# Program order on all engines through the chunked scan of a decoder layer: later tanh, exponentials in four parts, recurrence between the conv taps, sample-state product on GpSimd

## The chip, the cores and the metric

One NeuronCore of one Trainium2 chip runs the whole layer as one program. The metric is the device time in microseconds (us). The kernel before was run three times: 1119.72, 1119.86 and 1118.34 us, median 1119.72. Engines are called as in the profile: PE is TensorE, DVE is VectorE, ACT is ScalarE, POOL is GpSimd, SP is SyncE, whose queue issues nearly all DMAs.

## What is computed

One layer of a hybrid decoder for 512 prompt tokens and 8 single-token samples (520 columns in all), `D_MODEL` 1024. The part that matters is the input projection and the SSD branch:

```python
proj = h @ w_in                              # u | z | xBC | dt | gates
xbc  = silu(conv_b + sum_k full[:, k:k+L] * conv_w[k])     # 4 taps, causal
dt   = softplus(dt_raw + dt_bias);  dA = dt * A            # 32 heads
# chunks of 128 tokens, 8 groups of 4 heads, state 128, head width 64
Acs  = cumsum(dA);  decay = exp(tril(Acs[l] - Acs[s]))
y_diag = (C B^T * decay) @ (x * dt)
state  = B^T @ (exp(Acs[-1] - Acs) * x * dt);  h[c+1] = h[c] * exp(Acs[-1]) + state
y = y_diag + (C * exp(Acs)) @ h + D * x      # then gated by silu(z)
# samples: y_s = C . (ssm state) + ..., one step each
```

After it come the gates, the projection, the output projection and a SwiGLU FFN.

## The kernel before

Weights and activations are split into a high and a low part (`hi`, `lo`), and each product is three matmuls: hi*hi, hi*lo, lo*hi. A *column* is one 128-wide column of outputs: 8 row tiles x 3 products x 2 halves of 260 tokens = 48 matmuls into a two-bank PSUM tile `m` (`main()`, two buffers). For each column a weight tile of 128x1024 is loaded (`raw`, three buffers, SP queue), cast on ACT (`whi`, L116) and its remainder taken on DVE (`wlo`, L117). `plan` is a list of functions with their weights; `perform()` calls them in turn, having made the weights of two columns ahead (`LOOK`). PE's instructions stand in program order (`manual_schedule`). So do those of ACT, DVE and POOL, but only in `start()`, up to about 55 us of the span; behind it a scheduler orders ACT, DVE, POOL and SP by its own priorities, with `urgent()` as a boost.

The scan runs over 8 groups `g`. A group has four conv columns, `x0`, `x1` (the two x tiles, conv columns 2g and 2g+1), `bb` (B, 16+g) and `cc` (C, 24+g), and two gate columns `zz` of the group before (2g-2, 2g-1). Group 0's x0, x1 and the dt column are computed in `start()`. After a conv column `conv()` does this: ACT copies the PSUM tile to `xb` (L614) and writes `v` = last tap + bias (L615), which together free the PSUM tile; POOL clears three columns of `xb` (L610), keeps conv state (L616, L617) and adds the samples' part (L618); DVE adds three taps (L620); ACT takes tanh (L621); DVE writes the result `dst` (L622); POOL keeps its sample columns (L623). `v` and `t` have two buffers, `xb` three.

`ssd_open()` runs `dt_parts()` (softplus as a polynomial, 16 small DVE operations up to the cumulative sum `acs`, L543 to L556), stores `acs` to DRAM, and prepares `cpre` for the samples on POOL (L588, L590: five operations on 128x256, after the load of `cvs`). `dec_load(g)` loads `acs` broadcast to 128 partitions (`dec`, 1 MB). `scan(g)` is a generator whose parts are put between the columns of the next group: the exponentials (`cd`, `ce`, 16 Relu of 128x128, one Exp of 128x2048; L649 to L656) and C*exp (L658); transposes of x and B with `xdt`, `xde`, `bm` (L671 to L683); C B^T with mask and decay (L688 to L694); the chunk states and their recurrence on POOL and DVE (L702 to L715); the two y products (L727, L729); last the samples: a transpose of the sample B and C rows `bc_s` (L737), their store to `dbc`, loads of the state `h0` and of `cc`, and 16 fused multiply-and-sum operations `jk` on DVE (L749).

The PSUM buffers that set the order are these two pools; `main()` takes an `m` tile, `bank()` a `b` tile:

```python
    pm = ctx.enter_context(tc.tile_pool(name="pm", bufs=2, space=bass.MemoryType.PSUM))
    pb = ctx.enter_context(tc.tile_pool(name="pb", bufs=4, space=bass.MemoryType.PSUM))
```

## Time and profile before

| | |
|---|---|
| times of three runs | 1118.34, 1119.72, 1119.86 us |
| the profiled execution's own time | 1117.87 us |
| its span in the trace | 1116.1 us |
| PE, DVE, ACT, POOL busy | 1077.5, 699.5, 452.6, 318.2 us |
| DMA | 165.36 MB, mean 148 GB/s |
| stages on PE | start to 55.7 us; rest of the prologue and group 0 of the scan to 106.5; z columns of group 1 on to 383; pooling columns to 460; gates, projection, output to 740; FFN to 1116 |

The prediction reads four views. The page gives each engine's busy time. The *windows* view gives it for stretches of the span, with the clock that PE was granted. The *chain* is the work that ended last, followed back in time. The *timeline* and *lines* views give single instructions or groups: start, duration, engine, line, output<-inputs, shapes, and in brackets the idle time ahead of it and what ended that. Busy matmuls overlap their successor, so lost PE time is best read from start to start.

### The profile page before, as it was taken

To read this page: it belongs to the slowest core of one execution; us is meant where nothing else is said; L and a number is where in the kernel's file an instruction comes from. 1 tells how busy PE (TensorE), PEld (TensorE's weight loads), DVE (VectorE), ACT (ScalarE), POOL (GpSimd) and SP (SyncE) were. 2 spreads that over 40 slices of the span, in tenths; PEclk is the share of its full clock that TensorE was granted. 3 is DMA by queue.
4 is the path that set the end of the run, shared out by engine and by line. 5 is a ranking of instruction groups with operands and counts; after the bars stand their busy time and mean duration, and the time that the engine had idled before them with its cause. 6 is when DMAs were issued, how large, how long until landed. Compare 5 with 4: busy or idle time off the path is not lost.

```text
span 1116.1 us, 22431 instructions
## 1 busy us (share of the span) xinstructions
PE 1077.5 (97%) x9345; PEld 1047.7 (94%) x9345; DVE 699.5 (63%) x1203; ACT 452.6 (41%) x734; POOL 318.2 (29%) x482
## 2 busy tenths in 40 slices
PE   8999999999999899999999999999999999999995
PEld 6898989999999899999999999899999999999995
DVE  5687787687787887889677745657554553323332
ACT  3266554645545534665433323532222222222220
POOL 1154223122221222000000000399999950000001
PEclk8999999999999999999999999999999999999998
DMA  9535543444445332554335446267666652223212
GB/s 363 199 101 157 152 116 118 136 142 134 144 128 150 122 123 83 199 157 168 132 136 177 142 144 217 95 207 221 203 209 208 194 176 85 86 90 97 85 53 77
DMA packets 58470, 165.36 MB, mean 148 GB/s; under 512 B 10881, under 2 KB 16513, under 8 KB 57601
## 3 DMA queue, kind: packets, MB, share of 16 engines
q1 hardware_dynamic: 51712, 142.96, 39.4%
q0 software_dynamic: 6656, 20.98, 6.1%
q8 instruction: 73, 1.20, 0.4%
q14 instruction: 29, 0.23, 0.1%
HBM read 151.05 MB, written 12.86 MB: 147 GB/s over the span
## 4 chain that ended last, share of the span: by engine, by line
PE 70%; DMA 10%; DVE 8%; ACT 4%; issue 3%; POOL 3%; SPq 0%; DVEq 0%; ACTq 0%; POOLq 0%
PE m L129 62%; DMA dbc<-bcs 5%; DMA cc<-dbc 4%; PE b L129 4%; DVE v L620 3%; DVE jk L749 2%; ACT whi L116 1%; PE b L287 1%; PE b L193 1%; PE b L727 1%; DMA dec<-dacs 1%; DVE wlo L117 1%; ACT xb L614 1%; PE b L729 1%; POOL hst L714 0%
## 5 line engine op out<-in xcount | busy, mean ns | idle before, releaser
L129 PE MATMUL m<-hh,whi 128*128 128x260 f32 (+1 forms) x1840 | 381.1, 287 | 15.0 <-ACT v L615 12.9
L129 PE MATMUL m<-hl,whi 128*128 128x260 f32 (+1 forms) x1840 | 374.2, 283 | 3.3 <-DVE hl L467 3.1
L129 PE MATMUL m<-hh,wlo 128*128 128x260 f32 (+1 forms) x1840 | 373.8, 283 | 0.0
L117 DVE TENSOR_TENSOR wlo<-raw,whi 128x1024 fp32r<-128x1024 f32 (+2 forms) x169 | 229.7, 1361 | 152.5 <-ACT whi L116 148.8
L116 ACT CAST whi<-raw 128x1024 fp32r<-128x1024 f32 (+2 forms) x169 | 173.3, 1028 | 368.1 <-PE m L129 248.2
L129 PEld LDWEIGHTS m<-hh,whi 128*128 128x128 f32 x1840 | 285.4, 189 | 23.6 <-ACT v L615 15.8
L129 PEld LDWEIGHTS m<-hl,whi 128*128 128x128 f32 x1840 | 285.1, 189 | 4.4 <-DVE hl L467 4.0
L129 PEld LDWEIGHTS m<-hh,wlo 128*128 128x128 f32 x1840 | 285.5, 189 | 0.0
L327 POOL TENSOR_TENSOR r<-me,mhalf 128x5 f32<-128x5 f32 (+2 forms) x6 | 6.4, 1066 | 436.6 <-DVE me L326 436.6
L620 DVE SCALAR_TENSOR_TENSOR v<-xb,cwh,v 128x512 f32<-128x512 f32 x96 | 80.9, 843 | 24.7 <-ACT v L615 24.0
L621 ACT ACTIVATE t<-v 128x520 f32<-128x520 f32 x32 | 20.4, 639 | 112.9 <-DVE v L620 100.4
L129 PE MATMUL m<-ah,whi 128*128 128x260 f32 x264 | 53.2, 283 | 0.0
L129 PE MATMUL m<-ah,wlo 128*128 128x260 f32 x264 | 53.1, 282 | 0.0
L129 PE MATMUL m<-al,whi 128*128 128x260 f32 x264 | 53.0, 282 | 0.0
L129 PE MATMUL m<-gh,whi 128*128 128x260 f32 x256 | 52.8, 288 | 0.0
L129 PE MATMUL m<-gl,whi 128*128 128x260 f32 x256 | 51.3, 282 | 0.0
L129 PE MATMUL m<-gh,wlo 128*128 128x260 f32 x256 | 51.3, 282 | 0.0
L1180 DVE TENSOR_TENSOR fs<-m,fs 128x520 f32<-128x520 f32 (+2 forms) x23 | 15.5, 676 | 56.6 <-PE m L129 55.8
L1167 POOL TENSOR_TENSOR ht<-bb,xds 128x512 f32<-128x512 f32 x32 | 46.2, 1443 | 2.5 <-DMA bb<-dbc 2.0
L749 DVE SCALAR_TENSOR_TENSOR jk<-h,cc 128x128 f32<-128x128 f32 x128 | 37.5, 293 | 12.8 <-DMA cc<-dbc 11.5
L1169 POOL TENSOR_TENSOR hs<-hs,ht 128x512 f32<-128x512 f32 x32 | 44.5, 1389 | 0.8
L129 PEld LDWEIGHTS m<-gh,whi 128*128 128x128 f32 x256 | 39.2, 188 | 2.6 <-PE b L287 1.3
(297 smaller groups left out, 1721.1 us busy)
## 6 DMA issues: line engine op xcount, KB each, us to landing
raw<-in_win SPq DMA_DIRECT2D x73, 512.0 KB, 3.6
raw<-in_wfi SPq DMA_DIRECT2D x44, 512.0 KB, 4.4
araw<-in_wada SPq DMA_DIRECT2D x24, 512.0 KB, 4.1
h<-in_sssm SPq DMA_DIRECT2D x16, 512.0 KB, 4.1
raw<-in_wssd SPq DMA_DIRECT2D x16, 512.0 KB, 3.4
hs<-in_sssm POOLq DMA_DIRECT2D x32, 256.0 KB, 4.2
out_ssms<-hs POOLq DMA_DIRECT2D x32, 256.0 KB, 3.8
raw<-in_wfo SPq DMA_DIRECT2D x16, 512.0 KB, 3.5
```

What stands on the lines that cost most here:

```text
L116: nc.scalar.copy(hi, raw)
L117: nc.vector.tensor_tensor(lo, raw, hi.bitcast(F32), ALU.subtract)
L129: nc.tensor.matmul(o, a[:, k, c0 : c0 + P], b[:, t0:t1], start=f, stop=e)
L193: nc.tensor.matmul(ps[32 * i : 32 * i + 32, 0:n], sc[:, k], raw[:, n * i : n * i + n], start=first, stop=last)
L287: nc.tensor.matmul(ps[32 * i : 32 * i + 32, 0:256], scr[:, k], w[:, 256 * i : 256 * i + 256], start=k == 0 and j == 0, stop=k == KD - 1 an ...
L614: nc.scalar.copy(shape(xb[:, 3 + t0 : 3 + t1]), o)
L620: nc.vector.scalar_tensor_tensor(v[:, 0:TP], xb[:, k : k + TP], w(k), v[:, 0:TP], ALU.mult, ALU.add)
L621: nc.scalar.activation(t, v, AF.Tanh, bias=0.0, scale=1.0)
L749: nc.vector.scalar_tensor_tensor(jk, h0[:, i, j], 1.0, cc[:, i], ALU.mult, ALU.mult, accum_out=y_s[:, 2 * g + j, b + i : b + i + 1],)
L1167: nc.gpsimd.tensor_tensor(t, bb.unsqueeze(2).broadcast_to([P, 2, 2, P]), at(xds), ALU.mult)
L1169: nc.gpsimd.tensor_tensor(h, h, t, ALU.add)
L1180: nc.vector.tensor_tensor(view(s[:, t0:t1]), u, view(s[:, t0:t1]), ALU.mult)
```

## The change

Line numbers in the diff's own text are those of the two files; the changed file's lines are some 10 to 140 higher. It does seven things.

1. `manual_schedule` for PE, ACT, DVE and POOL holds from `start()` to the end of the scan's loop, and for SP from group 0's `cc` on. Everything there stands in the order of the calls.
2. `conv()` no longer ends its own column: tanh, `dst` and the sample copy go into `late`, and the next column's `conv()` or `gate()` runs them after its own PSUM reads and taps (`flush`).
3. The exponentials of a group are four pieces (`decays`), called from the `bb` column on; the even groups' `ce` lies in `aa`.
4. The chunk states follow the `bb` column, their POOL and DVE steps between its three taps (`mix`); the decay products (`scores`) are split in two.
5. The samples have a generator `sample(g)` of their own: the transpose of `bc_s` first, then per four samples a load, one 128x1024 product on POOL and one DVE reduction instead of eight `jk`.
6. `dt_parts` becomes a generator in three pieces, called in `ssd_open`, after x1 and after bb of group 0.
7. `ahead` loads the raw weights of two more columns, and `start()` casts the first two weights itself.

The core of the diff:

```diff
+    def ahead(n, m=0):
+        queue, made, raws = W["queue"], W["made"], W["raws"]
+        for i in range(len(made), min(n, len(queue))):
+            ...
+                raw = raws.pop(i) if i in raws else load(src)
+                made.append(parts(raw, pool))
+        for i in range(len(made), min(n + m, len(queue))):
+            ...
+                raws[i] = load(u[0] if isinstance(u, tuple) else u)
...
-            while len(made) < min(at + len(us) + (LOOK if at else 0), len(queue)):
-                u = queue[len(made)]
-                made.append(unit(*u) if isinstance(u, tuple) else unit(u))
+            ahead(at + len(us) + (LOOK if at else 0), W.get("loads", 0))
...
-        with urgent():
-            dt_parts(sp)
+        S["dt"] = dt_parts(sp)
+        next(S["dt"])
...
+        if mix:
+            next(mix)
         for k in range(3):
             nc.vector.scalar_tensor_tensor(v[:, 0:TP], xb[:, k : k + TP], w(k), v[:, 0:TP], ALU.mult, ALU.add)
-        nc.scalar.activation(t, v, AF.Tanh, bias=0.0, scale=1.0)
-        nc.vector.scalar_tensor_tensor(dst, t, 1.0, v, ALU.add, ALU.mult)
-        nc.gpsimd.tensor_copy(keep, dst[:, TP:T])
+            if mix:
+                next(mix)
+        flush()
+        def end():
+            nc.scalar.activation(t, v, AF.Tanh, bias=0.0, scale=1.0)
+            nc.vector.scalar_tensor_tensor(dst, t, 1.0, v, ALU.add, ALU.mult)
+            nc.gpsimd.tensor_copy(keep, dst[:, TP:T])
+        late.append(end)
...
+        for c in (0, 3, 2, 1):
+            if c:
+                nc.scalar.activation(ce[:, c - 1], dec[:, c], AF.Exp, bias=0.0, scale=1.0)
             for h in range(4):
                 a = tok[:, 1, c, 4 * g + h : 4 * g + h + 1]
                 nc.scalar.activation(dec[:, c, h], dec[:, c, h], AF.Relu, bias=a, scale=-1.0)
-        nc.scalar.activation(dec, dec, AF.Exp, bias=0.0, scale=-1.0)
+            nc.scalar.activation(dec[:, c], dec[:, c], AF.Exp, bias=0.0, scale=-1.0)
+            yield
...
+        nc.scalar.copy(hn[0], sv[0])
+        for c in range(1, 4):
+            nc.gpsimd.tensor_tensor(hn[c], hn[c - 1], cd[:, c].unsqueeze(2).broadcast_to([P, 4, 64]), ALU.mult)
+            yield
+            nc.vector.tensor_tensor(hn[c], hn[c], sv[c], ALU.add)
+        hst += hn
+        scores((2, 3) if g else range(4))
+        if not g:
+            decayed(g, ct)
...
+    def sample(g):
+        def mult(h0, cc):
+            nc.gpsimd.tensor_tensor(h0, h0, cc.unsqueeze(2).broadcast_to([P, 4, 2, P]), ALU.mult)
+        def sums(b, h0, cc):
+            out = y_s[:, 2 * g : 2 * g + 2, b : b + 4].rearrange("p j b -> p b j")
+            nc.vector.tensor_reduce(out, h0, axis=AX.X, op=ALU.add)
+        tb = bank()
+        nc.tensor.transpose(tb[0:16, 0:P], bc_s[:, g].rearrange("p a b -> p (a b)"), ident)
+        ...
+        yield
+        got = loads(0)
+        yield
+        mult(*got)
+        yield
+        sums(0, *got)
+        got = loads(4)
+        yield
+        mult(*got)
+        yield
+        sums(4, *got)
...
     for g in range(NG):
-        for fn, src in ((x0, X0), (x1, X1), (bb, BB), (cc, CC)):
...
+        todo(x0(g), *([X0(g)] if g else []))
+        if g > 1:
+            todo(step(g - 1))
+        if g:
+            todo(part(g - 1))
+        todo(x1(g), *([X1(g)] if g else []))
+        if g == 0:
+            todo(dt_more)
+        elif g == 1:
+            todo(decay(0, 2))
+            todo(step(0))
+            todo(step(0))
+        else:
+            todo(step(g - 1))
+        todo(bb(g), BB(g))
+        if g == 0:
+            todo(sp_order(True))
+            todo(dt_more)
+        else:
+            if g == 1:
+                todo(decay(0, 2))
+                todo(step(0))
+            todo(part(g - 1))
+            todo(decay(g))
+        todo(cc(g), CC(g))
+        if g:
+            todo(part(g - 1))
+            todo(decay(g))
             todo(zz(2 * g - 2), ZZ(2 * g - 2))
             todo(step(g - 1))
             todo(zend(2 * g - 2))
+            todo(part(g - 1))
+            todo(decay(g))
             todo(zz(2 * g - 1), ZZ(2 * g - 1))
             todo(step(g - 1))
-            todo(step(g - 1))
             todo(zend(2 * g - 1))
+            todo(part(g - 1))
+            todo(decay(g))
         todo(begin(g))
+        if g:
+            todo(part(g))
+        else:
+            todo(flush)
+            todo(part(0))
```

**ACT in the steady groups.** Before, in group 4, from the x1 column (conv column 9) to the B column (20); `t` is the tanh output, `hst` the first chunk state:

```order
L614 COPY xb9_2687<-m140_2638 128x520
L615 ACTIVATE v9_2688<-m140_2638,cwh_96 128x520
L621 ACTIVATE t9_2689<-v9_2688 128x520
L116 CAST whi148_2804<-raw147_2802 128x1024
L614 COPY xb20_2769<-m144_2720 128x520
L615 ACTIVATE v20_2770<-m144_2720,cwh_96 128x520
```

After, at the same place:

```order
L116 CAST whi145_2698<-raw136_2528 128x1024
L638 COPY xb20_2754<-m147_2705 128x520
L639 ACTIVATE v20_2755<-m147_2705,cwh_96 128x520
L759 COPY hst3_0_2769<-b148_2763 128x256
L652 ACTIVATE t9_2676<-v9_2675 128x520
L676 ACTIVATE cd4_2790<-dec4_2514 128x16
L687 ACTIVATE dec4_2514<-dec4_2514,tok_976 128x128 x4
L688 ACTIVATE dec4_2514<-dec4_2514 128x512
L116 CAST whi150_2797<-raw142_2623 128x1024
```

The tanh of column 9 stood ahead of the PSUM reads of column 20; now it stands behind them, followed by a quarter of the next group's exponentials.

**DVE at group 0.** Before, from the last small operations of dt to the C column's result (`ct0`):

```order
L554 TENSOR_SCALAR dtmp_620<-dtmp_620,ea_643 128x136
L563 COPY dds_652<-dtmp_620 32x8
L620 SCALAR_TENSOR_TENSOR v24_848<-xb24_847,cwh_96,v24_848 128x512
L556 SCALAR_TENSOR_TENSOR acs_646<-cst_75,dtmp_620 128x128
L622 SCALAR_TENSOR_TENSOR bt0_711<-t16_764,v16_763 128x520
L620 SCALAR_TENSOR_TENSOR v24_848<-xb24_847,cwh_96,v24_848 128x512 x2
L117 TENSOR_TENSOR wlo54_936<-raw53_933,whi54_935 128x1024
L620 SCALAR_TENSOR_TENSOR v2_919<-xb2_918,cwh_96,v2_919 128x512
L622 SCALAR_TENSOR_TENSOR ct0_797<-t24_849,v24_848 128x520
```

After, the same stretch; `wlo46` and `wlo49` are the weights of x0 and x1 of group 1:

```order
L568 TENSOR_SCALAR dtmp_633<-dtmp_633,ea_642 128x136
L570 SCALAR_TENSOR_TENSOR acs_700<-cst_75,dtmp_633 128x128
L646 SCALAR_TENSOR_TENSOR v16_754<-xb16_753,cwh_96,v16_754 128x512 x3
L653 SCALAR_TENSOR_TENSOR xg0_653<-t1_670,v1_669 128x520
L117 TENSOR_TENSOR wlo46_773<-raw45_770,whi46_772 128x1024
L578 COPY dds_784<-dtmp_633 32x8
L117 TENSOR_TENSOR wlo49_794<-raw47_776,whi49_793 128x1024
L646 SCALAR_TENSOR_TENSOR v24_850<-xb24_849,cwh_96,v24_850 128x512 x3
L653 SCALAR_TENSOR_TENSOR bt0_702<-t16_755,v16_754 128x520
L653 SCALAR_TENSOR_TENSOR ct0_799<-t24_851,v24_850 128x520
```

The dt chain no longer alternates with the taps; all taps of B and C and two weight remainders now stand behind it, and `ct0` last.

**PE at group 0.** Before, the end of the C column (`m49`) and the first matmuls of x0 of group 1 (`m52`):

```order
L129 MATMUL m49_798<-hh_101,whi44_781 128x260 x2
L129 MATMUL m49_798<-hl_102,whi44_781 128x260 x2
L129 MATMUL m49_798<-hh_101,wlo44_782 128x260 x2
L129 MATMUL m52_869<-hh_101,whi46_787 128x260 x2
L129 MATMUL m52_869<-hl_102,whi46_787 128x260 x2
```

After (`m51` is the C column, `m55` is x0 of group 1):

```order
L129 MATMUL m51_800<-hh_101,whi42_564 128x260 x2
L129 MATMUL m51_800<-hl_102,whi42_564 128x260 x2
L129 MATMUL m51_800<-hh_101,wlo42_565 128x260 x2
L806 MATMUL b52_870<-cst_75,bc_s_91 16x128
L129 MATMUL m55_882<-hh_101,whi46_772 128x260 x2
L129 MATMUL m55_882<-hl_102,whi46_772 128x260 x2
```

The transpose of group 0's sample rows (before at L737, behind group 0's second y product) now stands between the C column and x0.

On POOL the five `cpre` operations stood behind the three clears of `xb0`, `xb1` and `xb16`; now each clear stands behind them, in the order of the calls.

More of the change, by code (lines that the diff above doesn't have):

```diff
@@ L514, in start @@
         closed(st_)
-    def start_in_order():
-        E = mybir.EngineType
-        with tc.manual_schedule(engines={E.PE, E.Activation, E.DVE, E.Pool}):
-            start()
-    todo(start_in_order)
+    E = mybir.EngineType
+    ordered = tc.manual_schedule(engines={E.PE, E.Activation, E.DVE, E.Pool})
+    todo(lambda: ordered.__enter__() and None)
+    todo(start)
     S = {}
@@ L601, in tokens_dt, with flush, conv @@
         S["tok"] = tok
-    def conv(i, outs, dst, keep):
+    late = []
+    def flush():
+        for f in late:
+            f()
+        late.clear()
+    def conv(i, outs, dst, keep, mix=None):
         sp = S["sp"]
@@ L771, in tile_decoder, with sp_order, fn, step @@
     todo(ssd_open)
-    gens = {}
-    cur = {}
+    fetched = tc.manual_schedule(engines={E.SP})
+    def sp_order(on):
+        def fn():
+            if on:
+                fetched.__enter__()
+                W["loads"] = 2
+            else:
+                W["loads"] = 0
+                fetched.__exit__(None, None, None)
+        return fn
+    gens, samples, exps = {}, {}, {}
+    cur = {}
+    def step(g):
+        def fn():
+            next(gens[g], None)
+        return fn
+    def part(g):
+        def fn():
+            if g not in samples:
+                samples[g] = sample(g)
+            next(samples[g], None)
+        return fn
+    def decay(g, n=1):
+        def fn():
+            if g not in exps:
+                exps[g] = decays(g)
+            for _ in range(n):
+                next(exps[g], None)
+        return fn
+    def states_last():
+        for _ in range(4):
+            next(gens[7])
     def x0(g):
@@ L811, in fn @@
                 next(gens[g])
-        return fn
-    def step(g):
-        def fn():
-            next(gens[g], None)
         return fn
```

115 lines of the change are left out of this document (63 added, 52 removed).

## The prediction

> **What bounds the kernel now.** First the page: PE is busy nearly all the time, so only idle or slowed PE time can be won. The windows view says where it lies, the chain what an undisturbed stretch takes, the waits and the timeline who is late.
>
> ```profile
> PE 1077.5 (97%) x9345; PEld 1047.7 (94%) x9345; DVE 699.5 (63%) x1203; ACT 452.6 (41%) x734; POOL 318.2 (29%) x482
> 106.50:375.50 269.00, 256.68 (x2238) 250.19 (x2238) 205.72 (x441) 137.62 (x251) 67.57 (x163) 0.99 0.44 134
> 383.50:460.00 76.50, 76.50 (x659) 75.64 (x658) 62.32 (x169) 34.47 (x63) 14.86 (x28) 1.00 0.37 124
> ```
>
> In the steady scan (second row) PE lacks 12.3 us of 269; behind 383 us, where the edit's remainder lies, it lacks nothing, and there I count the edit at nothing: columns stand wall to wall there. Start to start says a little more, since a restart also costs something that shows as busy. From the chain:
>
> ```profile
> 106.50 7.31 PE m L129 x48
> ...
> 375.55 6.02 PE m L129 x48
> ...
> 383.46 5.76 PE m L129 x48
> ...
> 404.68 7.20 PE m L129 x60
> ...
> 413.32 5.76 PE m L129 x48
> 419.09 1.02 PE b L727 x16
> ...
> 420.77 5.95 PE m L129 x48
> ...
> 428.40 1.64 PE m L129 x12
> ```
>
> A group is six columns, the transposes, C B^T, the states and two y products. Undisturbed: three columns with transposes, C B^T and states 404.68 - 383.46 = 21.22; a column 419.09 - 413.32 = 5.77; two columns with their y product 7.45 (to 420.77) and 7.63 (to 428.40). Together 42.07. The six groups from the last gate column of group 1 (106.50) to that of group 7 (375.55) took 269.05, undisturbed 252.4: 16.6 us are lost, 1.5 of them in the slow column at 106.50 (7.31 for 5.8, treated below). So **15.1 us** is all that the steady groups can give.
>
> ```profile
> PE m L129 <- ACT v L615: 12.4, 11, 2.0
> ACT t L621 <- DVE v L620: 92.6, 23, 7.2
> 186.64 0.64 ACT L621 ACTIVATE t<-v 128x520 f32<-128x520 f32 x1 [6.51 <-DVE v L620]
> 187.18 1.03 ACT L116 CAST whi<-raw 128x1024 fp32r<-128x1024 f32 x1
> 188.12 0.58 ACT L614 COPY xb<-m 128x520 f32<-128x520 f32 x1
> 188.60 0.79 ACT L615 ACTIVATE v<-m,cwh 128x520 f32<-128x520 f32 x1
> 189.44 0.51 PE L129 MATMUL m<-hh,whi 128*128 128x260 f32 x2 [2.01 <-ACT v L615]
> ```
>
> The first two rows are the waits from 115.4 to 383.2 us. ACT, in order, sits 6.5 us before a tanh whose taps are late on DVE; the PSUM reads behind it come late, and PE waits 2.0 us for a free `m` tile. Eleven waits end so, 12.4 us.
>
> **The steady part of the change.** With tanh behind the next column's PSUM reads, ACT no longer waits there. Does something else come late? ACT gets per group what it had (137.62 / 6 = 22.9 us in 42); its longest step, a column with a quarter of the exponentials, is cast 1.03, reads 1.2, tanh 0.6, pieces 2.2, some 5 us against columns of 5.8 and more. DVE loses the 16 `jk` of a group and their waits for `cc`, and gets two reductions:
>
> ```profile
> L749 DVE SCALAR_TENSOR_TENSOR jk<-h,cc 128x128 f32<-128x128 f32 x96 | 27.8, 290 | 9.7 <-DMA cc<-dbc 8.7
> L1167 POOL TENSOR_TENSOR ht<-bb,xds 128x512 f32<-128x512 f32 x32 | 46.2, 1443 | 2.5 <-DMA bb<-dbc 2.0
> 191.56 1.11 DVE L620 SCALAR_TENSOR_TENSOR v<-xb,cwh,v 128x512 f32<-128x512 f32 x1
> SPq L745 <- DMA dbc<-bcs: 48.5, 8, 8.2
> ```
>
> 16 x 0.29 = 4.6 us go; no row has the reduction, its nearest, a 128x1024 `wlo` (1.22, below), gives 2.4; so DVE has about 32 of 42 us (205.72 / 6 = 34.3 before). POOL gets two products of 128x1024, 2 x 2 x 1.44 = 5.8 us, on top of 67.57 / 6 = 11.3: room enough. The third row, a tap that took 1.11 beside POOL's recurrence step, where others take 0.74, says that the two engines hinder each other; at worst the 5.8 us are added to DVE's 32, 38 of 42. On SP the `cc` load waits up to 8.2 us for `dbc`, with weight loads queued behind it; they are now issued two columns (11.6 us) ahead, which covers that. I take all 15.1; bounds 7.5 (waits left in every second group) and 15.1.
>
> The Trainium skill, GPSIMD Engine Reference (Engine selection; Key points), speaks against such a product: elementwise work on GpSimd is about 2x slower than on VectorE, and it shares SBUF interfaces with VectorE instructions that have two SBUF inputs. The 1.11 us row agrees with the second; by the page's 4497 ns for 2048 elements the product would take some 2.2 us (an estimate), not 2.9, and the sum stays as it is.
>
> **The fill.** Here the order of the calls costs. Group 0's C column ends on PE at 67.2, and x0 of group 1 follows at once:
>
> ```profile
> 67.20 0.40 PE L129 MATMUL m<-hh,whi 128*128 128x260 f32 x2
> 80.33 0.93 PE L671 MATMUL b<-cst,xg 128*128 128x128 f32 x7
> 59.43 0.74 POOL L588 TENSOR_TENSOR cpre<-cvs,cwh 128x256 f32<-128x256 f32 x1 [0.15 <-DMA cvs<-in_sconv]
> 108.42 2.32 DVE L620 SCALAR_TENSOR_TENSOR v<-xb,cwh,v 128x512 f32<-128x512 f32 x3
> 59.06 1.00 DVE L544 RECIPROCAL dtmp<-dtmp 128x136 f32<-128x136 f32 x1
> 70.78 0.29 DVE L549 SCALAR_TENSOR_TENSOR dtmp<-dtmp 128x136 f32<-128x136 f32 x1
> 70.99 0.69 DVE L622 SCALAR_TENSOR_TENSOR xg<-t,v 128x520 f32<-128x520 f32 x1
> 75.64 0.41 DVE L556 TENSOR_TENSOR_SCAN acs<-cst,dtmp 128x128 f32<-128x128 f32 x1
> 83.93 1.22 DVE L117 TENSOR_TENSOR wlo<-raw,whi 128x1024 fp32r<-128x1024 f32 x1
> 68.30 0.20 POOL L623 COPY xs_s<-xg 128x8 f32<-128x8 f32 x1 [0.94 <-DVE xg L622]
> ```
>
> After the change the transpose of `bc_s` stands ahead of x0, and it needs `ct0`, the last of a row of DVE work in strict order. From `cvs` at 59.43: five POOL operations of 0.74, then the clear of `xb0`: 63.3. Taps of x0 and x1, 2.25 each until the next can start: 67.8. x0's result 0.62 (0.69 less overlap): 68.4. The dt chain, 16 dependent operations: 1.00, 0.41, a small 0.23 and 13 of 0.29, with 0.04 between dependent ones (2.32 for three taps of 0.74): 6.0, to 74.4. Taps of B 2.25, x1's result 0.62, two `wlo` with the small `dds` 2.4: 79.7. Taps of C 2.32, tanh 0.64, `ct0` 0.69, POOL's copy 0.2 and hand-overs: **83.7**. Queued behind the waiting transpose is all of PE; it stands **16.5 us** where it stood not at all. ACT's own queue (PSUM reads, `whi46`, `whi49`) is through before DVE needs it. Bounds 14.5 (dependent operations at 0.21 spacing, as 70.78 to 70.99) and 18 (1.5 us more in POOL's steps and the hand-overs). The two casts that `start()` now makes itself cost nothing: PE has work there, and they end by 56, before the C column reads the second.
>
> PE's clock comes on top:
>
> ```profile
> 102.60:106.00 3.40, 1.94 (x26) 1.16 (x26) 2.23 (x6) 3.40 (x8) 2.33 (x5) 1.00 0.00 0
> 106.00:109.40 3.40, 3.40 (x17) 3.07 (x18) 2.86 (x5) 0.30 (x1) 2.09 (x2) 0.50 0.39 118
> ```
>
> After a 3.4 us stretch with 1.94 us of work, the next 3.4 us had half the clock: that was the 1.5 us of the column at 106.50. A restart after 16 us falls somewhere inside such a stretch, so between one and two of them are slow: 1.5 to 3.4 us, I take 2.2. So x0 ends at 83.7 + 5.8 + 2.2 = 91.7, and x1 with its token transposes (5.8 + 0.3) at **97.8**, where before it ended at 80.33: 17.5 us later.
>
> The Trainium skill, TensorE: Matmul & The Clock Gate (Part 1), has the clock drop after at least one idle window of about 3.4 us and return after one busy one. The row at 102.60 was no idle window, and the clock dropped all the same; by the page's rule the slow column of 106.50 need not come again (rival D).
>
> From the end of x1 to the z1 column (the second gate column) of group 1, before took 106.50 - 80.33 = 26.2. Now ACT sets it:
>
> ```profile
> 117.07 3.62 ACT L655 ACTIVATE aa<-aa,tok 128x128 f32<-128x128 f32 x12
> 123.41 1.90 ACT L656 ACTIVATE aa<-aa 128x2048 f32<-128x2048 f32 x1
> 115.53 1.50 ACT L651 ACTIVATE ce<-aa 128x1536 f32<-128x1536 f32 x1 [0.38 <-PE b L729]
> L714 POOL TENSOR_TENSOR hst<-hst,cd 128x256 f32<-128x256 f32 x21 | 14.2, 675 | 10.0 <-DVE hst L715 10.0
> L715 DVE TENSOR_TENSOR hst<-hst,b 128x256 f32<-128x256 f32 x21 | 8.7, 414 | 5.8 <-POOL hst L714 5.8
> 82.29 8.10 DMA dec<-dacs
> ```
>
> Behind x1's column ACT has three PSUM reads of 1.25, two tanh 1.2, two casts 2.0, a copy 0.5 (a 128x520 one had 0.58), and five pieces of exponentials: 20 Relu of 0.30, five Exp and three `ce` of 0.5, two `cd`, 10.3. Together 17.8, and C's reads come last. Then the recurrence among the taps, a half-size copy 0.35, 3 x (0.61 + 0.42 + 0.12), in all 3.8, four score products and three `ce` products at 0.6 = 4.2, the last y matmuls 0.3: **26.1**. PE alone needs 21.22 - 5.8 + 7.45 = 22.9: a wait of 3.2 before z1, so z1 has the slow clock again, as at 106.50. `dec` is no bound: its load stands on SP behind `wlo46` (78.4), the stores and seven loads, leaves at about 87.5 and lands 8.1 later, 4 us before its first reader. So z1 starts 17.5 + 26.1 - 26.2 = **17.4 us** later.
>
> **The sum.** +17.4 - 15.1 = **+2.3 us**. On the profiled execution's own time, 1117.87 (span 1116.1), that is 1120.2. It lies 1.85 below the median of the runs, 1119.72, on whose scale the forecast is **1122.0**. About 0.2% (2.2 us) is what a measurement here can tell from no change; the forecast stands on that line, on the slow side.
>
> **Rivals.**
> A. The fill costs less, not slower. DVE starts dependent small operations at 0.21 instead of 0.33 us (16 of them, -1.9) and the clock takes one slow stretch (-0.7): +2.3 - 2.6 = -0.3, 1119.4. For it: the spacing at 70.78. Against it: there another operation stood between. It decides where x0 starts before 81.4; under 0.2% faster needs 79.2.
> B. GpSimd's products hold DVE up, and PE keeps a wait in every second group: 7.5 instead of 15.1, +9.9, 1129.6. For it: 1.11 against 0.74 us. Against it: 38 of 42 us at worst, and every deadline of DVE is a column or two away. By the skill's GPSIMD page this is the way that it would go; so far one row speaks for it.
> C. ACT's reads are late for another cause: `v` has two buffers, so its write waits for the result of the column before last, now one column later on DVE. I count 0.7 us of margin at `cc`; with none, the waits go on (1.1 us in each of the six groups): +6.6, +8.9, 1128.6.
>
> D. The clock stays full behind the second wait: 3.2 us need not make one whole stretch idle. Then z1 takes 5.8 and not 7.3: +2.3 - 1.5 = +0.8, 1120.5. Against it: 1.94 of 3.40 us were enough at 102.60.
>
> **Chances.** Forecast (fill +16 to +19, groups -14 to -15) 0.45, its own range 1120 to 1124, half on either side of 1122; A 0.20; D 0.08; B or C 0.20; something else 0.07. Range: lower end A with 2 us more from the fill, 1117.5; upper end between C and B, 1129. Faster by over 0.2%: half of A and some, 0.13. Same: half of the forecast, half of A, D, 0.42. Slower: half of the forecast, B and C and some, 0.45.
>
> **What would show it.** Right: a PE gap of about 16 us at 67 us, ended by POOL's copy of `ct0`; x0 of group 1 at 83.7; a clock of 0.5 behind it; a PE wait of about 3 us ahead of group 1's z1, ended by DVE's `ce`; from there group periods of 42.1 with no wait for `v`. Wrong: x0 starting before 80 us, or waits for ACT or DVE above 0.5 us left in groups 2 to 7.

## The result and the profile after

The changed kernel took 1130.92 us (median of four runs, 1130.63 to 1131.66), the kernel before, run beside it, 1119.79 us (1118.34 to 1121.06). The ratio is 1.0101, 95% interval 1.0083 to 1.0118: 1% slower. The forecast was 1122.0, with 1117.5 to 1129.0 as its range, so the time lies above the range.

Of the profiled execution of after (span 1129.1 us), the page's row of busy times and four rows of the windows view (window, its length, then busy time with instructions of PE, weight loads, DVE, ACT and POOL, the granted clock, DMA share, GB/s):

```profile
PE 1078.7 (96%) x9345; PEld 1050.5 (93%) x9345; DVE 697.6 (62%) x963; ACT 465.1 (41%) x774; POOL 349.2 (31%) x498
67.00:83.00 16.00, 0.00 (x0) 0.00 (x0) 15.19 (x30) 6.62 (x12) 4.08 (x11) 0.63 0.04 6
120.00:130.00 10.00, 2.24 (x16) 1.21 (x16) 7.46 (x12) 6.65 (x13) 4.21 (x6) 0.61 0.04 14
141.36:394.92 253.56, 253.56 (x2240) 248.57 (x2239) 199.04 (x257) 146.36 (x279) 95.34 (x179) 1.00 0.47 142
374.10:460.00 85.90, 85.90 (x764) 84.44 (x763) 71.37 (x120) 40.63 (x76) 32.70 (x47) 1.00 0.36 119
```

PE now stands idle twice, from 67 to 83 us and around 120 us, and nowhere in the six steady groups (third window). Before, six groups cut at the same place had 12.4 us of idle PE:

```profile
115.41:383.19 267.78, 255.41 (x2241) 248.93 (x2240) 204.12 (x439) 138.57 (x252) 67.76 (x164) 1.00 0.45 135
```

To compare runs, I cut the span at three places on PE: the end of group 0's C column, and the sample transposes that end the column work of group 1 and of group 7 (115.41 and 383.19 us before, 141.36 and 394.92 after; the C column ends at 67.20 and 66.30). *Fill* is from the first to the second, *six groups* from the second to the third, *rest* from there to the end of the span. All runs, experiments included, in us:

| kernel | fill | six groups | rest | span | ratio to before (95% interval) |
|---|---|---|---|---|---|
| before | 48.2 | 267.8 | 732.9 | 1116.1 | |
| after | 75.1 | 253.6 | 734.2 | 1129.1 | 1.0101 (1.0083 to 1.0118) |
| late_rows | 69.5 | 253.6 | 735.9 | 1127.3 | 1.0038 (1.0021 to 1.0055) |
| dt_own | 69.0 | 253.6 | 733.3 | 1121.8 | 1.0028 (1.0013 to 1.0043) |
| both_moves | 69.0 | 253.6 | 733.6 | 1121.9 | 1.0022 (1.0005 to 1.0040) |
| clears_first | 66.2 | 253.6 | 733.3 | 1120.4 | 1.0026 (1.0011 to 1.0041) |
| free_fill | 58.7 | 253.6 | 732.8 | 1112.5 | 0.9934 (0.9914 to 0.9955) |
| free_fill2 | 51.3 | 253.6 | 733.5 | 1105.5 | 0.9893 (0.9873 to 0.9913) |
| early_tanh | 81.6 | 256.5 | 737.6 | 1144.4 | 1.0221 (1.0193 to 1.0250) |
| whole_exps | 77.6 | 253.6 | 731.9 | 1128.4 | 1.0114 (1.0088 to 1.0141) |
| sched_all | 65.2 | 269.0 | 732.7 | 1133.0 | 1.0116 (1.0082 to 1.0149) |
| dve_product | 75.0 | 253.6 | 734.3 | 1130.1 | 1.0098 (1.0069 to 1.0127) |
| after_again | 75.2 | 253.6 | 734.4 | 1128.9 | 1.0102 (1.0073 to 1.0132) |
| warm | 74.7 | 253.6 | 733.1 | 1130.3 | one time, 1132.29 us |
| order_dve | 73.3 | 274.8 | 735.3 | 1149.4 | one time, 1151.20 us |
| order_act | 71.8 | 262.4 | 733.1 | 1133.5 | one time, 1135.73 us |

From before to after: fill +26.9, six groups -14.2, rest +1.3, start -0.9, in all +13.0 us of span. (The medians differ by 11.1, since the profiled execution of before was 1.85 us below its median.) Where a time is given *on the first scale*, it is the ratio times 1119.72 us, the median of the first three runs of before. The rest varies from 731.9 to 737.6 us over kernels that are alike there, so its +1.3 means nothing. What the groups gained, the fill lost nearly twice.

The fill of after in the timeline (start, duration, instruction, in brackets the idle time ahead and what ended it):

```profile
82.39 0.70 DVE L653 SCALAR_TENSOR_TENSOR ct<-t,v 128x520 f32<-128x520 f32 x1 [0.15 <-ACT t L652]
83.40 0.38 PE L806 MATMUL b<-cst,bc_s 128*16 128x128 f32 x1 [16.94 <-POOL xb L634]
93.86 0.38 SPq L668 DMA_DIRECT2D dec<-dacs  x1
102.25 0.23 ACT L676 ACTIVATE cd<-dec 128x16 f32<-128x16 f32 x1 [2.74 <-DMA dec<-dacs]
110.04 1.05 ACT L116 CAST whi<-raw 128x1024 fp32r<-128x1024 f32 x1 [2.60 <-DMA raw<-in_win]
```

Group 0's C result is made at 82.39, and the transpose of the sample rows starts at 83.40 after 16.94 us of idle PE, as forecast. Then something that was not forecast. The waits (who, for whom, total, times, longest), SP's queue first:

```profile
SPq L668 <- PE b L614: 9.0, 1, 9.0
PE b L778 <- DVE dec L742: 8.9, 1, 8.9
```

SP has the load of the first decays (`dec`) at its head and holds it for 9.0 us, until PE has transposed dt (L614, in the middle of x1). It leaves at 93.86, and ACT, in order, first waits 2.74 us for it, then 2.60 us for the weights of the first gate column, which were sent behind 2 MB of decays. The chain (start, duration, what) goes on from there:

```profile
120.82 0.50 ACT xb L638
...
127.02 0.70 DVE dec L742
127.72 0.04 issue
127.76 2.50 PE b L778 x16
130.26 1.80 PE b L780 x12
132.07 7.68 PE m L129 x48
```

The PSUM reads of group 1's C column (L638) come some 9.5 us after PE has finished it, DVE's recurrence and decay products behind them, and PE waits 8.9 us ahead of the first y product (L778).

### The profile page after: what moved, and what is told of

It is laid out like the page before. It is cut to its first block, busy times and chain, and to the rows that moved or that the text cites. A ratio compares the mean times of both kernels' runs of the same rounds, so it can differ in the third digit from the quotient of the medians.

```text
span 1129.1 us, 22192 instructions
## 1 busy us (share of the span) xinstructions
PE 1078.7 (96%) x9345; PEld 1050.5 (93%) x9345; DVE 697.6 (62%) x963; ACT 465.1 (41%) x774; POOL 349.2 (31%) x498
## 4 chain that ended last, share of the span: by engine, by line
PE 88%; DVE 4%; issue 2%; DMA 2%; ACT 2%; POOL 1%; SPq 0%; DVEq 0%; POOLq 0%; ACTq 0%
PE m L129 77%; PE b L129 4%; PE b L778 2%; DMA raw<-in_win 1%; PE b L756 1%; PE b L780 1%; PE b L301 1%; DVE v L646 1%; PE b L734 1%; PE b L207 1%; PE b L717 1%; DVE acc L391 0%; DMA xT<-in_xT 0%; DMA raw<-in_wada 0%; POOL xn L1219 0%
## 5 line engine op out<-in xcount | busy, mean ns | idle before, releaser
L117 DVE TENSOR_TENSOR wlo<-raw,whi 128x1024 fp32r<-128x1024 f32 (+2 forms) x169 | 234.0, 1387 | 151.1 <-ACT whi L116 148.3
L646 DVE SCALAR_TENSOR_TENSOR v<-xb,cwh,v 128x512 f32<-128x512 f32 x96 | 72.9, 760 | 52.8 <-ACT v L639 30.2
L1323 DVE TENSOR_TENSOR fs<-m,fs 128x520 f32<-128x520 f32 (+2 forms) x23 | 15.4, 675 | 70.6 <-PE m L129 69.8
L638 ACT COPY xb<-m 128x520 f32<-128x520 f32 (+1 forms) x31 | 17.9, 577 | 93.4 <-PE m L129 93.4
L129 PE MATMUL m<-gl,whi 128*128 128x260 f32 x256 | 51.3, 282 | 0.0
L129 PE MATMUL m<-gh,wlo 128*128 128x260 f32 x256 | 51.3, 282 | 0.0
L1312 POOL TENSOR_TENSOR hs<-hs,ht 128x512 f32<-128x512 f32 x32 | 47.8, 1494 | 0.8
L799 POOL TENSOR_TENSOR h<-h,cc 128x1024 f32<-128x1024 f32 x16 | 38.3, 2395 | 25.2 <-DMA cc<-dbc 24.2
L1310 POOL TENSOR_TENSOR ht<-bb,xds 128x512 f32<-128x512 f32 x32 | 41.0, 1282 | 2.2 <-DMA bb<-dbc 1.7
```

Source lines behind the costliest of these rows:

```text
L117: nc.vector.tensor_tensor(lo, raw, hi.bitcast(F32), ALU.subtract)
L129: nc.tensor.matmul(o, a[:, k, c0 : c0 + P], b[:, t0:t1], start=f, stop=e)
L638: nc.scalar.copy(shape(xb[:, 3 + t0 : 3 + t1]), o)
L646: nc.vector.scalar_tensor_tensor(v[:, 0:TP], xb[:, k : k + TP], w(k), v[:, 0:TP], ALU.mult, ALU.add)
L799: nc.gpsimd.tensor_tensor(h0, h0, cc.unsqueeze(2).broadcast_to([P, 4, 2, P]), ALU.mult)
L1310: nc.gpsimd.tensor_tensor(t, bb.unsqueeze(2).broadcast_to([P, 2, 2, P]), at(xds), ALU.mult)
```

## The experiments

The theory that I held after reading the trace of after (F): the fill is set by two chains, the transposed sample rows and the load of the decays. Its rivals are named with each run.

**1. The sample transpose moved behind x1 (late_rows).** Group 0's call goes; group 1 makes it up:

```diff
             todo(flush)
-            todo(part(0))
...
         elif g == 1:
+            todo(part(0))
+            todo(part(0))
             todo(decay(0, 2))
```

> The kernel after, but with group 0's sample transpose called behind x1 of group 1 instead of ahead of its x0. Theory F (two chains set the fill: the transposed rows, and behind them the broadcast load of the decays, which cannot leave before SP has sent the dt stores, about 85 us, and lands some 8.4 us later): x0 of group 1 starts at 66.5 us, but x1 now waits for the C column's PSUM reads (some 5 us), and the decays come at 93.5 instead of 102.25 us, so the second gate column of group 1 starts only 8 to 10 us earlier than 132.0; time 1121 to 1123 us. Rival G (the 16.9 us stall is simply taken out, with the 2 us of slow clock behind it): 1111 to 1114 us. Rival H (the DVE row is all that counts, whatever PE does meanwhile): within 2 us of 1130.9.

Measured: 1.0038 (1.0021 to 1.0055), on the first scale 1124.0 us; the fill 5.6 us shorter. The profiled execution, 1129.34 us, was the slowest of ten (1121.58 to 1129.34); its C column ended 2.1 us later than after's. Neither theory F's 8 to 10 us nor G's 19 came out. PE's waits from 60 to 140 us (total, times, longest):

```profile
PE b L778 <- DVE dec L742: 9.4, 1, 9.4
PE m L129 <- DVE wlo L117: 5.8, 1, 5.8
PE m L129 <- ACT whi L116: 4.6, 1, 4.6
```

The transpose is gone from the list, but x0 now waits for its own weights: their cast on ACT (4.6 us) and their remainder on DVE (5.8 us) stand in strict order behind the tanhs, the dt chain and the taps. Of the 16.9 us, 10.4 were thus waiting that x0 would have done in the transpose's place. By the time F came nearest, 1 us above its range, but not for its reason: it let x0 start at 66.5 us and run through, and x0 started at 73.14 and stood again until 80.22. Rival H (no gain) is out by its time; what it has right is that DVE's row holds PE up without the transpose too.

**2. Memory of their own for dt's temporaries (dt_own).** They lay in the buffer that the first decays are loaded into:

```diff
-        tmps = sp.tile([P, 9, 136], F32, tag="dec", name="dtmp")
+        tmps = sp.tile([P, 9, 136], F32, tag="ce", name="dtmp")
```

> The kernel after, but with the temporaries of dt in the memory of ce instead of that of dec, so that the first load of the decays need not wait for the transposes of dt on PE (93.6 us). The stall at 67 us stays in every theory. Theory F: the load leaves at about 85 us and lands at 93.5, ACT's waits of 2.74 us for dec and 2.60 us for the weights behind it go, and PE's second wait, 8.9 us, falls to about 3.5; time 1124.5 to 1127 us. Rival A (the second wait is ACT's own work and the recurrence, as strict order puts them; the load only shows up as its releaser): 1129.5 to 1131.5 us.

Measured: 1.0028 (1.0013 to 1.0043), on the first scale 1122.9 us. SP's row in the timeline:

```profile
84.40 0.58 SPq L668 DMA_DIRECT2D dec<-dacs  x1
```

and PE's waits from 60 to 140 us:

```profile
PE b L806 <- POOL xb L634: 16.7, 1, 16.7
PE b L778 <- DVE dec L742: 3.6, 2, 3.4
```

The load leaves 9.5 us earlier, ACT's two waits for DMA are gone, PE's second wait falls from 8.9 to 3.4, and the fill is 6.1 us shorter; the interval lies wholly below that of after. Theory F stands, with a gain somewhat above the one it gave (1122.9 against 1124.5 to 1127); rival A falls.

**3. Both edits (both_moves).**

> The kernel after with both edits, the late transpose and dt's temporaries in ce. Theory F: with the transposes of dt on PE at 80 us the load is bound by SP's queue (85 us) either way, so this is no faster than the late transpose alone by more than 1 us: 1120 to 1123 us. Rival G: 1106 to 1110 us, the sum of two separate gains (19 and 5 us).

Measured: 1.0022 (1.0005 to 1.0040), the fill 69.0 us: no more than either edit alone, as F expected. The second wait is back, 8.9 us, because what comes earlier on PE finds ACT waiting for weights that were sent in the same rush (7.6 us for `raw`).

**4. POOL's clears ahead of cpre (clears_first, on dt_own).** The first three `xb` tiles are cleared in `ssd_open()`.

```diff
+        S["xb"] = [sp.tile([P, 16 + T], F32, tag="xb", name=f"xb{i}", bufs=3)[:, 13:] for i in (0, 1, 16)]
+        for xb in S["xb"]:
+            nc.gpsimd.memset(xb[:, 0:3], 0.0)
         cpre = sp.tile([P, 32, NS], F32, name="cpre")
```

> The kernel of the dt_own run, with the clears of the first three xb tiles ahead of the five cpre operations on POOL. Theory F (the chain at the fill starts with POOL: cpre 59.2 to 63.1 us, clear, then DVE's row in strict order up to the C result): DVE's taps start at about 58.5 instead of 63.15 us, the stall ahead of the sample transpose falls from 16.9 to 12.5 us, and with the dt stores the load of the decays comes earlier too: second gate column at 121 to 122.5 us instead of 126.1, time 1119 to 1121.5 us on the scale of the first runs (ratio 0.998 to 1.001). Rival K (the cvs load or cpre bounds the sample columns, which tanh needs as well): no gain, ratio 1.002 to 1.004.

Measured: 1.0026 (1.0011 to 1.0041), the same as dt_own. DVE's taps and POOL's `cpre` now run side by side. The timeline of this run:

```profile
60.31 6.25 DVE L653 SCALAR_TENSOR_TENSOR v<-xb,cwh,v 128x512 f32<-128x512 f32 x6 [2.03 <-ACT v L646]
60.58 1.19 POOL L607 TENSOR_TENSOR ctmp<-cvs,cwh 128x256 f32<-128x256 f32 x1
64.15 1.07 POOL L609 TENSOR_TENSOR cpre<-cpre,ctmp 128x256 f32<-128x256 f32 x1
66.66 0.64 ACT L659 ACTIVATE t<-v 128x520 f32<-128x520 f32 x1 [4.99 <-POOL v L649]
```

and the same taps and the last `cpre` step in after:

```profile
62.33 0.74 POOL L606 TENSOR_TENSOR cpre<-cpre,ctmp 128x256 f32<-128x256 f32 x1
63.15 4.58 DVE L646 SCALAR_TENSOR_TENSOR v<-xb,cwh,v 128x512 f32<-128x512 f32 x6 [5.90 <-POOL xb L634]
```

The six taps start 2.8 us earlier but take 6.25 us instead of 4.58 and end only 1.2 us earlier, POOL's steps 1.07 and more instead of 0.74, and tanh waits 4.99 us for POOL's sample columns. Rival K holds in the times. The fill of the one traced execution is still 2.8 us shorter; the ratio does not show that.

**5. The scheduler's order kept through group 1 (free_fill).** Program order on ACT, DVE, POOL and SP begins at group 2, with edits 1 and 2.

```diff
     todo(start)
+    todo(lambda: ordered.__exit__(None, None, None) and None)
...
     for g in range(NG):
+        if g == 2:
+            todo(lambda: again.append(tc.manual_schedule(engines={E.PE, E.Activation, E.DVE, E.Pool})) or again[0].__enter__() and None)
+            todo(sp_order(True))
         todo(x0(g), *([X0(g)] if g else []))
```

> The kernel after with both edits, and with ACT, DVE, POOL and SP left to the scheduler from the end of the prologue until group 2, where program order is taken up again. Theory F: the fill ends about where it did before (second gate column of group 1 at 105 to 109 us) and the steady groups keep periods of 42.3 us, 13.8 us less than before in all: 1105 to 1110 us. Rival S (the steady gain needs the order of the fill too, for the loads that it issues ahead): waits return in groups 2 to 7, 1112 to 1120 us.

Measured: 0.9934 (0.9914 to 0.9955), on the first scale 1112.3 us: faster than both kernels, but not the 1105 to 1110 expected. The six groups kept all their gain, so rival S falls; the fill was 58.7 us, not 48. The waits up to group 1's end, two rows of PE and one of DVE, say why:

```profile
PE b L780 <- DVE dec L744: 5.7, 1, 5.7
PE b L616 <- POOL bc_s L656: 4.0, 1, 4.0
DVE y_s L805 <- POOL h L801: 6.1, 1, 6.1
```

The dt chain had lost its priority (before it was `urgent()`), and DVE stood 6.1 us before the sum of group 0's samples, waiting for GpSimd's product, with group 0's last decay product and the C column's taps behind it.

**6. The same, with these two taken out (free_fill2).** dt is urgent again, and group 0's sample products run beside the last pooling and gate columns.

```diff
+        with urgent():
+            next(S["dt"])
...
-        if t < 5:
-            todo(part(7))
+        todo(part(7 if t < 5 else 0))
```

> The kernel with the scheduler's order through group 1 (as the free_fill run), with three further moves: the small dt operations are urgent again, as before the change, the sample transpose of group 0 is called behind x1 of group 1 and its products of state and C come behind the scan, beside the last pooling and gate columns. Theory F: the wait of 4.3 us for the dt chain and the one of 5.7 us in the y products, in which DVE stood 6.1 us for GpSimd's product, go for the most part, and with them some slow clock: second gate column at 105 to 111 us instead of 117.5; 1103 to 1109 us by the scale of the first three runs of before (ratio 0.985 to 0.990). Rival D (the broadcast load of the decays, 2 MB in front of the weights, bounds the fill in any order): at 114 to 118 us, ratio 0.991 to 0.995.

Measured: 0.9893 (0.9873 to 0.9913), 1107.7 us on the first scale: the fastest of all, 1.1% below before. PE's waits from 60 to 130 us, the longest two groups:

```profile
PE b L783 <- DVE hst L766: 2.1, 2, 1.1
PE b L809 <- POOL bc_s L657: 1.5, 1, 1.5
```

and the six groups in the windows view:

```profile
118.39:371.95 253.56, 253.56 (x2240) 248.56 (x2238) 195.11 (x254) 144.06 (x274) 96.20 (x178) 1.00 0.46 138
```

No wait above 1.5 us is left in the fill, and the groups keep their gain. Rival D falls: the 2 MB of decays are loaded here too.

**7. Tanh early again (early_tanh).**

```diff
-        late.append(end)
+        end()
```

> The kernel after, but each conv column ends itself: tanh, result and sample copy in its own conv(), ahead of the next column's PSUM reads, as before; all else stays in program order. Theory L (the late tanh is what took the waits for v out of the steady groups): PE waits for ACT's reads return in groups 2 to 7, 0.5 to 2 us in a group, and the groups from z1 of group 1 to z1 of group 7 take 257 to 266 us instead of 255.3; time 1133 to 1142 us. Rival P (program order with the exponentials in pieces does it, whichever side tanh stands on): 1129.5 to 1132.5 us, no waits.

Measured: 1.0221 (1.0193 to 1.0250), on the first scale 1144.5 us, above both theories, but the loss is not where theory L put it. The fill took 81.6 us, 6.5 more, since DVE's row now has a wait for tanh behind each column (5.4 us of such waits up to 150 us, 0.2 in after). The six groups took 256.5 us, 2.9 more. From z1 to z1, as L counts, they took 258.2, near the lower end of its 257 to 266; but the waits that L named did not return. ACT's waits in the six groups, and PE's from 140 to 430 us:

```profile
ACT t L652 <- DVE v L646: 105.9, 24, 6.3
PE m L129 <- DVE gz L830: 2.0, 3, 0.8
PE b L727 <- DVE y L784: 1.0, 1, 1.0
PE m L129 <- DVE wlo L117: 0.6, 1, 0.6
```

ACT waits ahead of tanh for even longer than before the change (92.6 us), and yet no PE wait for ACT's reads is among the rows: in the six groups PE waits 2.0 us for DVE's results (`gz` 1.4, `wlo` 0.6), and the first three groups take 42.26 us each as in after. In the groups a late tanh is worth 2.9 of the 14.2 us, no more; L is right that it counts, and wrong in how.

**8. The exponentials in one block (whole_exps).**

```diff
-            for _ in range(n):
+            for _ in range(4):
                 next(exps[g], None)
```

> The kernel after, but the four pieces of a group's exponentials are issued at one place, behind the B column's reads (about 10 us of ACT work in one block ahead of the C column's reads). Theory E (the pieces are needed): the reads of the C column come some 5 us late, waits of 1 to 3 us in each group, 1135 to 1150 us. Rival P2 (two PSUM buffers hide a block of 10 us, since the tile is needed only a column later): 1129 to 1132.5 us.

Measured: 1.0114 (1.0088 to 1.0141), not to be told from after; the six groups 253.6 us. Rival P2 holds: two PSUM buffers hide a block of 10 us, and the spreading was worth nothing in the steady groups.

**9. All new call places, but the scheduler's order (sched_all).**

```diff
     todo(start)
+    todo(lambda: ordered.__exit__(None, None, None) and None)
...
             if on:
-                fetched.__enter__()
                 W["loads"] = 2
```

> The kernel after with all its new places of calls, but with program order on ACT, DVE, POOL and SP ending with the prologue, as before the change; behind it the scheduler sorts them. Since the run with the early tanh kept nearly all of the steady gain (256.5 instead of 253.6 us for the six groups from the sample transpose of group 1 to that of group 7; 267.8 before), theory P says that program order gives the gain: here waits of ACT's reads come back, and the six groups take 262 to 270 us. Rival L2 (the late tanh and the new places of the calls give it, sorted or not): 253.5 to 256 us. The fill keeps the stall for the sample transpose in both.

Measured: 1.0116 (1.0082 to 1.0149); the six groups took 269.0 us, as long as before the change. PE's and ACT's waits in them:

```profile
PE m L129 <- ACT v L640: 10.8, 6, 2.4
ACT cd L677 <- DMA dec<-dacs: 23.6, 3, 8.2
```

With late tanh, four pieces and the GpSimd product all in place, the gain is nil. Theory P holds in this: without program order there is no gain. Whether order alone is enough is not shown: the old places of the calls were not run in program order, and the early tanh, the one block and DVE's product were each tried alone. Of the 26.9 us that the fill lost, 17.0 are lost in this run too; PE waits 11.0 us there ahead of the sample transpose, 3.8 for ACT's reads and 2.1 in the y products. Order itself thus costs the fill about 10 us (75.1 against 65.2 here, 69.0 in both_moves against 58.7 in free_fill).

**10. Program order on one engine (order_dve, order_act).** As sched_all, with the order kept behind the prologue on DVE or on ACT alone (the first is shown).

```diff
+    todo(lambda: one.append(tc.manual_schedule(engines={E.PE, E.DVE})) or one[0].__enter__() and None)
```

> The kernel of the sched_all run, but with program order kept on DVE (and PE) through the scan; ACT, POOL and SP are sorted by the scheduler. Theory V (the waits of the steady groups came from DVE's order: other work between the taps of a column keeps tanh and with it the next reads waiting, 6.5 us before the change, 3.6 to 4.1 in program order with the early tanh): the six groups from the sample transpose of group 1 to that of group 7 take 253.5 to 258 us. Rival T (ACT's order is what counts): 264 to 270 us, as in the sched_all run (269.0).

> The kernel of the sched_all run, but with program order kept on ACT (and PE) through the scan; DVE, POOL and SP are sorted by the scheduler. Rival T: the six groups take 253.5 to 258 us. Theory V: the waits stay, 262 to 270 us.

Measured, one time each: 274.8 us for the six groups with DVE's order, 262.4 with ACT's. Both theories fall. ACT's longest waits in them with order on DVE:

```profile
ACT cd L679 <- DMA dec<-dacs: 34.7, 3, 13.3
ACT cd L679 <- DMA aa<-dacs: 30.9, 3, 10.8
```

and with order on ACT (not counting those for PE's columns):

```profile
ACT v L642 <- DVE xg L656: 42.4, 10, 7.1
```

With DVE's order alone ACT stands up to 13.3 us before the decays, whose loads SP sends late; with ACT's alone it stands up to 7.1 us before DVE's result, which frees the buffer of `v`. Of the 15.4 us between sched_all and after, ACT's order alone brought 6.6, DVE's alone none; all of it came only with every queue in order. Which further queue brings the remainder stays open: POOL's and SP's orders were not tried by themselves.

**11. The product on DVE (dve_product).**

```diff
-            nc.gpsimd.tensor_tensor(h0, h0, cc.unsqueeze(2).broadcast_to([P, 4, 2, P]), ALU.mult)
+            nc.vector.tensor_tensor(h0, h0, cc.unsqueeze(2).broadcast_to([P, 4, 2, P]), ALU.mult)
```

> The kernel after, with the samples' two products of 128x1024 in a group on DVE instead of GpSimd. Theory F (nothing off PE's fill chain counts, and DVE has slack in the groups): six groups at 253.6 us, no waits, time within 2 us of the kernel after. Rival B (GpSimd's product beside DVE costs DVE time in the fill, where DVE's row bounds): 2 to 4 us faster. Rival B2 (DVE gets too full): waits in the groups, slower by 3 us or more.

Measured: 1.0098 (1.0069 to 1.0127): no difference. The six groups in the windows view, where DVE has the room:

```profile
142.26:395.82 253.56, 253.56 (x2240) 248.56 (x2239) 206.39 (x270) 146.35 (x280) 74.15 (x167) 1.00 0.48 143
```

**12. PE kept busy in the wait (warm).**

```diff
+        for _ in range(110 if g == 0 else 0):
+            nc.tensor.matmul(tb[:, 0:H2], hh[:, 0, 0:P], hh[:, 0, 0:H2], start=True, stop=True)
         nc.tensor.transpose(tb[0:16, 0:P], bc_s[:, g].rearrange("p a b -> p (a b)"), ident)
```

> The kernel after, with 110 matmuls of 128x260 (some 13 us) put ahead of group 0's sample transpose, whose results nobody reads, so that PE is busy in most of the 16.9 us wait. Theory C (the half clock behind the wait is due to PE's idle time): the clock stays at 1.0 through x0 and x1 of group 1, which with the token transposes take 12.0 us instead of 14.1, and the second gate column comes about 2 us earlier. Rival C2 (the clock goes down for another reason at that place): still half clock up to about 88 us, 14.1 us.

Measured: one time, 1132.29 us. The start of x0 in the windows view, first in after:

```profile
83.00:86.40 3.40, 3.00 (x15) 3.00 (x16) 1.32 (x2) 1.20 (x2) 0.22 (x2) 0.50 0.49 28
86.40:89.80 3.40, 3.40 (x23) 3.40 (x23) 0.00 (x0) 0.00 (x0) 0.00 (x0) 0.74 0.51 163
```

then in this run:

```profile
85.90:89.30 3.40, 3.40 (x21) 3.40 (x22) 1.23 (x1) 1.20 (x2) 0.00 (x0) 0.69 0.42 29
89.30:92.70 3.40, 3.40 (x26) 3.40 (x25) 0.00 (x0) 0.00 (x0) 0.00 (x0) 0.81 0.48 157
```

and PE's wait that was left:

```profile
PE b L808 <- POOL xb L634: 3.7, 1, 3.7
```

The clock still falls, but elsewhere. In windows of 0.5 us it is 1.00 up to 87.0, past the restart at 85.9, and 0.50 from 87.5 to 90.5; in after it fell at 71.1, inside the wait, and came back at 88.2. So the fall follows PE's idle time, as theory C has it, and rival C2 falls. That less idle time leaves less slow clock behind it is not shown: x0 and x1 with their transposes took 13.5 us here and 14.1 in after, but also 13.5 in early_tanh and 13.2 in clears_first, behind 21.4 and 15.6 us of idle PE. The 0.4 us by which the fill is shorter than in after are within the scatter of other traces with this fill (75.0 in dve_product, 75.2 in after_again).

**13. After once more (after_again).**

> The kernel after, unchanged, on the chip of these runs, so that the others have it beside them: every theory expects a ratio to before of 1.008 to 1.012.

Measured: 1.0102 (1.0073 to 1.0132).

## Why the prediction was wrong, point by point

**The fill up to x1** was right, nearly to the number: x0 of group 1 at 83.43 us (forecast 83.7), idle PE 16.9 us (16.5), the loss to slow clock 14.1 - 12.0 = 2.1 us (2.2), x1 with its transposes done at 97.5 (97.8). One thing in it was only argued and half wrong: that PE waits because of the transpose. The late_rows run shows that x0's own weights would have held it for 10.4 of the 16.9 us.

**The step that failed** is the sentence "`dec` is no bound: its load stands on SP behind `wlo46` (78.4), the stores and seven loads, leaves at about 87.5 and lands 8.1 later, 4 us before its first reader". It counted the queue ahead of the load and not the buffer that the load writes. That buffer held dt's temporaries, which PE's transposes (L614) read last, and these transposes moved with x1, from 75.15 us before to 93.56. The load left at 93.86, landed 2.74 us after ACT wanted it, and pushed the next weights another 2.60 us late. From the end of x1 to z1 it took 34.5 us and not 26.1. The dt_own run takes that alone away, and the second wait falls from 8.9 to 3.4 us, where the forecast had 3.2; it is worth 6.1 us. From the end of x1 to z1 it takes 29.0 us there, of which 2.6 are the next point: the 26.1 that I added up for ACT and the recurrence were right within 0.3.

**A second term was too small:** slow clock behind the second wait. I charged z1 1.5 us; it took 7.68 for 5.95, 1.7. But the y products ahead of it ran at half clock too, 4.2 us for 1.67, and I charged them nothing: 2.6 us.

```profile
123.40:126.80 3.40, 0.00 (x0) 0.00 (x0) 2.28 (x5) 3.29 (x7) 2.18 (x3) 0.50 0.00 0
126.80:130.20 3.40, 2.44 (x16) 1.21 (x16) 3.40 (x7) 0.00 (x0) 0.00 (x0) 0.50 0.13 41
130.20:133.60 3.40, 3.40 (x21) 2.52 (x20) 3.40 (x5) 1.54 (x4) 0.19 (x1) 0.50 0.02 5
133.60:137.00 3.40, 3.40 (x22) 3.40 (x21) 3.37 (x6) 2.46 (x6) 0.31 (x2) 0.66 0.75 199
```

These are windows of after. The clock stayed at half through 130.20 to 133.60, a row with 3.40 of 3.40 us busy; 0.66 in the next means half clock for 2.3 of its 3.4 us, up to 135.9. The Trainium skill, TensorE: Matmul & The Clock Gate (Part 1), has the clock back after at least one busy window of some 3.4 us. Behind the first wait the trace agrees with that (0.74 from 86.40 on means half clock up to 88.2, 4.8 us behind the restart); here 8.1 us passed from the restart at 127.76. In dt_own it was 7.2 us behind a wait of 3.4. Why it took longer there than behind the first wait is not shown. Rival D, a full clock there, is refuted.

**The steady groups:** the size was right and the reason mostly wrong. z1 of group 1 to z1 of group 7 took 255.3 us, 13.8 less than before; the forecast had 15.1. An undisturbed group is 42.26 us, not the 42.07 that I put together from chain pieces, six times 0.19. But the reason given, that tanh behind the reads takes ACT's wait away, is worth 2.9 us (early_tanh), and the pieces of exponentials nothing (whole_exps); without program order the gain is zero (sched_all). The row that misled me, ACT waiting 6.51 us ahead of a tanh, was a true wait. What made it that long was other work between the three taps of that column on DVE (181.31, 182.57 and 185.79 us): C B^T's mask, two decay products and a `jk` that stood for its load:

```profile
185.58 0.29 DVE L749 SCALAR_TENSOR_TENSOR jk<-h,cc 128x128 f32<-128x128 f32 x1 [1.66 <-DMA cc<-dbc]
```

In program order with the early tanh ACT waits as often and up to 6.3 us, and PE does not wait for its reads.

**The sum:** +2.3 forecast. z1 of group 1 came at 132.0 us instead of 123.9 (106.50 + 17.4), 8.1 late: 5.7 from the longer second wait (8.9 for 3.2), 2.6 from the slow y products, less 0.3 at x1. The groups gave 1.3 less, and behind z1 of group 7 came another 1.3, within the scatter of the rest. Together 13.0, as measured from trace to trace.

**The rivals.** A (a cheaper fill) is refuted. B (GpSimd's products hold DVE up) is refuted in the groups: no wait is left there, and on DVE the product gives the same 253.6 us. A wait for these products can cost PE all the same, in the fill: in free_fill DVE stood 6.1 us for one, and PE 5.7 us behind it. C (`v`'s two buffers) is refuted for this order, and appears with up to 7.1 us when ACT alone is ordered. No rival had the load of the decays. The Trainium skill, GPSIMD Engine Reference (Engine selection; Key points), spoke against the product; here it took 2.40 us on GpSimd, near the 2.2 estimated from the page, and 1.22 on DVE (dve_product), and the page's shared interfaces show in clears_first (0.74 to 1.07 us), but neither set the time:

```profile
L799 POOL TENSOR_TENSOR h<-h,cc 128x1024 f32<-128x1024 f32 x12 | 28.8, 2400 | 21.3 <-DMA cc<-dbc 21.3
```

## What to carry to other kernels

For a load that is moved or whose surroundings move, ask when its destination becomes free, not only when the queue reaches it: the last reader of whatever shared that memory can be on another engine and may have moved too. Program order can pay in the steady loop and cost in the fill of the same kernel; price the two apart, and start it where the pipeline is full. When a strict row is late, taking away the instruction that is seen to wait gains only up to the next one that depends on the same row.

## What the runs showed of the hardware that was not expected

Two engines side by side gained little from overlap: six taps on DVE beside POOL's `cpre` took 6.25 us instead of 4.58, and the `cpre` steps 1.07 to 1.19 instead of 0.74, so that of a start 2.8 us earlier 1.2 were left at the end of the taps. And PE's clock came back 4.8 us behind one wait (16.9 us idle, columns behind it) and 8.1 us behind a shorter one (8.9 us idle, y products behind it).
